# Two attentions with transposed value products, an output product with one sum per attention, and later value transposes in the delta rule

## Chip, cores and metric

The kernel runs on 1 core of one Trainium2 chip. The metric is the device time of one execution in microseconds (us), the median over runs; lower is better. All times are of this one core.

## The reference

Two transformer layers run one after the other on 256 tokens of width 1024, all in float32. What the change touches:

```python
h = rmsnorm(x, g_mix_pre); proj = h @ w_in
y_fox = forgetting_attention(fq, fk, fv, f_logit)            # 8 heads of 64
y_chk = chunked_relpos_attention(cq, ck, cv, rel_bias)       # 8 heads of 64
y = concat([rmsnorm(y_fox.reshape(S, 512), g_fox_out), rmsnorm(y_chk.reshape(S, 512), g_chk_out)])
x = x + rmsnorm(y @ w_out, g_mix_post)
h = rmsnorm(x, g_mem_pre)
x = x + rmsnorm(memory_cross_attention(h, mem_n, ...), g_mem_post)   # 4 heads of 256, ends with @ w_mo
h = rmsnorm(x, g_ff_pre); x = x + rmsnorm(square(relu(h @ w_ff1)) @ w_ff2, g_ff_post)
```

Both attentions of the first line are causal: a softmax over at most 256 keys, then probabilities times values. The second layer has a chunked gated delta rule (8 heads of 128, two chunks of 128 here), an indexer with top-k that masks a second attention (8 heads of 128, named DSA below), gates, an output product and a feed-forward part.

## The kernel before

Every large product is split into three float32r matmuls (`mm3`: high part by high part, high by low, low by high). The stationary and moving operands are tiles with 128 partitions; tokens are handled as two halves of 128 (`A` and `B` in the code, half 0 and half 1). Weights come in units of 512 KB by a DMA from the SP queue into `raw`; ScalarE (ACT) casts `whi`, VectorE (DVE) subtracts to `wlo`. Products with names `gt` give a transposed result (features on partitions, 256 columns), `gn`, `gs` and `mo` a natural one (tokens on partitions, 512 columns), `acc` is the second feed-forward product.

The order of the instructions is made while the program is written out. `Kern` keeps a modelled clock of TensorE and modelled end times of the other engines. Small chains of work (attention heads, norms, evacuations) are generators, called sides. A side yields the tiles it needs, a number of us to wait, a bank of PSUM, or other sides. After each piece of a product `tick` (L261) lets those sides go on whose inputs the model says are ready; `finish` (L272) empties sides at once, whether or not their inputs are near. The result is a fixed order on each engine, which the chip then follows with semaphores. PSUM has 8 banks, and `nb` counts them.

The places that the change and the prediction touch, by the names of the code:

- `attn_pv` (L671): per head three fp32 products with the transposed probabilities `pt` (128x128) stationary and the head's 64 value columns moving, into the natural bank `o`. In the trace each fp32 product has two records.
- `head_pairs` (L862): for two heads at a time scores, softmax, three transposes of `p` (`tb<-ident,p`), a copy `pt` on DVE, then `attn_pv`.
- `out_norm` (L842), once per attention: divides `o` by the softmax sums, squares for the norm, scales by the gain, and four transposes per half (`tb<-ident,y`) through `chain_xt` to the split operand `yt`.
- Output product: `gemm_n_skew(k, yt, 2, ev, ...)` (L990), names `gs`; its post chain `chain_post` (L498) makes the norm, the residual sum `x`, the next norm's `xg` and eight transposes per half (`tb<-ident,xg`) into `xb`. The memory's value product `gemm_n_inter` (`gn`, L991) follows, and then the query product of the memory attention (`gt`).
- Memory attention `mem_head`: scores `ms`, transposes of `mp`, the copy `mpt`, value products `ops`, split `xhi`, `xlo`; then the product with `w_mo` (`mo`, L1043 on).
- Second layer: `chain_v` transposes the values `vc`; `gdn` and `gdn_o` are the delta rule (`wp`, `kp`, `qp`, `op_`), which run among the heads of DSA (`s`, `p`, `pt`, `ao`).

Of the kernel before, what the change touches and what calls it, by code (L numbers as in the profile page):

```python
# [38 lines left out]
def hs(half):  # L39
    return slice(half * P, half * P + P)  # L40
# [454 lines left out]
    yield from chain_xt(k, xt, half, xg, rs)  # L495


def chain_post(k, half, y, gpost, x_old, x_new, gpre, xt):  # L498


    nc = k.nc
    c = lambda t, j: t[:, j * 512:j * 512 + 512]
    yield y
    if gpost is not None:
        ss = mean_sq(k, y, D)
        yg = k.t4([P, D], name="yg")
        for j in range(2):
            nc.vector.tensor_tensor(c(yg, j), y[j], c(gpost, j), op=OP.mult)
        k.put(2)
# [17 lines left out]
    yield rs  # L527
    yield from chain_xt(k, xt, half, [c(xg, 0), c(xg, 1)], rs)


# [178 lines left out]
def block1(k, x, mem, w_in, b_fgt, rel, g_fox_out, g_chk_out, w_out, g_mix_pre, g_mix_post,  # L709
# [123 lines left out]
    gemm_t(k, ht, 512, ev)  # L833


    y = [k.t4([P, D], name="y") for _ in range(2)]
    yt = XS(k)
    gfc = k.t4([P, 2, 512], name="gfc")
# [3 lines left out]
    def out_norm(o, sums, col, g):  # L842

        def half(qt):
            yy = y[qt][:, col:col + 512]
            rs = k.small(8, "rsum")
            nc.vector.reciprocal(rs, sums[:, qt])
            nc.vector.tensor_tensor(yy.rearrange("p (h d) -> p h d", h=8),
                                    o[qt].rearrange("p (h d) -> p h d", h=8), bc(rs, 64), op=OP.mult)
            k.put()  # L850
            ss = mean_sq(k, [yy[:, :256], yy[:, 256:]], 512)
            nc.vector.tensor_tensor(yy, yy, g, op=OP.mult)
            yield ss
            r = rstd_col(k, ss, 512)
            yield r
            yield from chain_xt(k, yt, qt, [yy], r, col // 512)
        yield from join([k.add(half(qt), rank=0) for qt in range(2)])

    def hs64(j):
        return slice(j * 64, j * 64 + 64)  # L860

    def head_pairs(scores, weights, v, o):  # L862
        def rest(h, s):
            p = yield from weights(h, s)
            pt = yield from attn_transpose(k, p, nc.vector.tensor_copy)
            c = slice(h * 64, h * 64 + 64)
            attn_pv(k, pt, v[:, 0, c], v[:, 1, c], o[0][:, c], o[1][:, c])

        def pair(i):
            s = yield from scores(i)  # L870
            yield from join([k.add(rest(2 * i + j, s[j])) for j in range(2)])
        return lanes(k, pair, 4, 3)

    def fox():
        yield from join([s_f])
        o = []
        for _ in range(2):
            o.append((yield from k.get(name="o")))
        sums = k.keep([P, 2, 8], "fsums")

        def scores(i):

            yield fq[:, i], fk[:, i]
            s = []
            for _ in range(2):
                s.append((yield from k.get((P, 4, P), "s")))
            for j in range(2):
                k.mm(flat(s[j])[:, 0:384], sel[:, 2 * i + j], flat(ncum), True, False)
                k.mm(s[j][:, 0], k.identb, k.maskb, False, False)
                k.mm(s[j][:, 2], k.identb, k.maskb, False, False)  # L890
            for j in range(2):
                hp = hs64(j)
                k.mm(s[j][:, 0], fq[hp, i, :P], fk[hp, i, :P], False, False)
            for j in range(2):
                hp = hs64(j)
                k.mm(flat(s[j])[:, P:384], fq[hp, i, P:], fk[hp, i], False, True)
            return s

        def weights(h, s):
            yield s  # L900
            nmx = k.small(2, "nmx")
            nc.vector.tensor_reduce(nmx[:, 0:1], s[:, 0], AX.X, OP.max, negate=True)
            nc.vector.tensor_reduce(nmx[:, 1:2], flat(s)[:, P:384], AX.X, OP.max, negate=True)
            p = k.t2([P, 3, P], name="p")
            softmax_exp(k, p, s, nmx, sums, h)
            k.put()
            return p

        yield from join(head_pairs(scores, weights, fv, o))
        yield o  # L910
        yield from out_norm(o, sums, 0, gfc[:, 0])

    s_fox = k.add(fox())

# [12 lines left out]
    def chk():  # L927
        o = []
        for _ in range(2):
            o.append((yield from k.get(name="o")))  # L930
        sums = k.keep([P, 2, 8], "csums")

        def scores(i):
            yield cq[:, i], ck[:, i]
            s = []
            for _ in range(2):
                s.append((yield from k.get((P, 4, P), "s")))
            for j in range(2):
                hp = hs64(j)
                k.mm(s[j][:, 0], cq[hp, i, :P], ck[hp, i, :P])  # L940
            for j in range(2):
                hp = hs64(j)
                k.mm(flat(s[j])[:, P:384], cq[hp, i, P:], ck[hp, i])
            return s

        def weights(h, s):
            r = rb[h // 4][:, h % 4]
            yield s
            mx = k.small(2, "mx")
            lg = k.t2([P, 3, P], name="lg")  # L950
            nc.vector.tensor_tensor_reduce(lg[:, 0], s[:, 0], r[:, P:], 1.0, 2 * NEG, OP.add, OP.max, mx[:, 0:1])
            nc.vector.tensor_tensor_reduce(flat(lg)[:, P:], flat(s)[:, P:384], r, 1.0, 2 * NEG, OP.add, OP.max,
                                           mx[:, 1:2])
            k.put()
            nmx = k.small(2, "nmx")
            nc.vector.tensor_scalar(nmx, mx, -1.0, None, op0=OP.mult)
            p = k.t2([P, 3, P], name="p")
            softmax_exp(k, p, lg, nmx, sums, h)
            return p

        yield from join(head_pairs(scores, weights, cv, o))
        yield o
        yield from out_norm(o, sums, 512, gfc[:, 1])

    s_chk = k.add(chk())

# [19 lines left out]

    x1 = x0
    ht = XT(k)
    ev, st = post_chain(gpo, x0, x1, gmp, ht)
# [50 lines left out]
    x2 = x1  # L1040
    ht = XT(k)
    ev, st2 = post_chain(gmo, x1, x2, gfp, ht)
    parts = {}  # L1043
    for half in range(2):
        ps = [k.bank(name="mo") for _ in range(2)]
        for js, iis in ((0, (0, 1, 2)), (1, (0, 1, 2)), (0, (3,)), (1, (3,))):
            if iis == (3,):
                k.finish(st[3])
            for i in iis:
                if half == 0:  # L1050
                    while (js, i) not in parts:
                        n = len(parts)
                        parts[n // 4, n % 4] = k.part()
                        k.held += 1
                else:
                    k.drop()
                mm_n(k, ps[js:js + 1], ot, half, parts[js, i], 2 * i)
        ev(half, 0, ps[0:1])
        ev(half, 1, ps[1:2])


    gfo2, gnx = gain(k, g_ff_post), gain(k, next_gain)
# [105 lines left out]
def block2(k, x3, ht, st, out, conv_w, norm_mlp_g):  # L1168
# [735 lines left out]
```

## Time and profile before

| what | value |
|---|---|
| median of 3 runs | 884.3 us (883.33 to 884.74) |
| the profiled execution itself | 884.03 us |
| its span from first to last instruction | 882.1 us |
| mean granted clock of TensorE | 1.000 |
| PE (matmuls) busy | 870.4 us, 99% |
| DVE busy | 603.5 us, 68% |
| ACT busy | 465.3 us, 53% |
| POOL busy | 89.2 us, 10% |

An engine's idle time costs only where TensorE then waits. A matmul's busy time runs past the start of the next one, since matmuls are pipelined; what a matmul costs the program is the distance from its start to the start of the next one, and that is how the rows of a timeline are read here.

### The profile page before, as it was taken

The page shows a single profiled execution, that of the slowest core. Times are in us where ns is not written, and L with a number is a line of the kernel's source. Part 1 is how long each engine was busy: PE and PEld are TensorE (multiplying, and loading weights), DVE is VectorE, ACT ScalarE, POOL GpSimd, SP SyncE. Part 2 cuts the span into 40 slices and gives each one's busy share as a digit, 9 for nine tenths or more (in the row PEclk, how much of TensorE's full clock was granted, in tenths as well). Part 3 has the DMA queues.
Part 4 walks back from the last instruction along what each step waited for, and adds up shares of the span by engine and source line. Part 5 has one row for each costly group of instructions (what it writes and reads, how often), then busy time and mean ns, then how long its engine had stood idle before and what let it go on. Part 6 is the DMA issues. An engine that isn't in the chain of part 4 may idle for free.

```text
span 882.1 us, 13900 instructions
## 1 busy us (share of the span) xinstructions
PE 870.4 (99%) x5320; PEld 754.0 (85%) x5320; DVE 603.5 (68%) x1061; ACT 465.3 (53%) x837; POOL 89.2 (10%) x148
## 2 busy tenths in 40 slices
PE   7999999999999999999999999999999999999998
PEld 6979998799788888888798899988977888888887
DVE  5675664765687667664768999879567786666661
ACT  6574654554476444443648664553765564444440
POOL 3100010200020000000100138600010000000000
PEclk9999999999999999999999999999999999999999
DMA  8982436473387666654553586485235587666521
GB/s 268 294 246 77 144 120 239 119 262 99 94 242 218 207 201 191 191 191 146 172 161 97 143 188 182 97 230 155 71 95 173 165 252 200 191 191 191 192 96 48
DMA packets 162612, 150.82 MB, mean 171 GB/s; under 512 B 20081, under 2 KB 127217, under 8 KB 162546
## 3 DMA queue, kind: packets, MB, share of 16 engines
q1 hardware_dynamic: 161970, 148.88, 56.9%
q10 hardware_dynamic: 576, 1.05, 0.4%
q8 instruction: 42, 0.69, 0.3%
q14 instruction: 24, 0.20, 0.1%
HBM read 148.08 MB, written 1.84 MB: 170 GB/s over the span
## 4 chain that ended last, share of the span: by engine, by line
PE 90%; DVE 4%; ACT 4%; DMA 1%; issue 1%; POOL 0%; ACTq 0%; DVEq 0%; POOLq 0%
PE gt L212 33%; PE acc L212 20%; PE gn L212 12%; PE gs L212 11%; PE tb L225 3%; PE mo L212 3%; DVE wlo L96 2%; PE o L212 1%; ACT whi L96 1%; PE s L212 1%; PE ops L212 1%; PE ms L212 1%; ACT p L96 1%; DMA raw<-in_w_out_dram 1%; PE qp L212 1%
## 5 line engine op out<-in xcount | busy, mean ns | idle before, releaser
L96 DVE TENSOR_TENSOR wlo<-raw,whi 128x1024 fp32r<-128x1024 f32 (+1 forms) x263 | 315.9, 1224 | 107.9 <-ACT whi L96 98.8
L96 ACT CAST whi<-raw 128x1024 fp32r<-128x1024 f32 (+1 forms) x264 | 269.4, 1048 | 61.0 <-DMA raw<-in_w_in_dram 28.8
L212 PE MATMUL gt<-xb,whi 128*128 128x256 f32 (+1 forms) x1152 | 276.1, 322 | 0.0
L212 PE MATMUL gt<-xb,wlo 128*128 128x256 f32 x768 | 215.0, 280 | 0.0
L212 PEld LDWEIGHTS gt<-xb,whi 128*128 128x128 f32 x1152 | 189.9, 188 | 17.2 <-issue 0.3
L212 PEld LDWEIGHTS gt<-xb,wlo 128*128 128x128 f32 x768 | 144.7, 188 | 0.3
L212 PE MATMUL acc<-wlo,uh 128*128 128x512 f32 (+1 forms) x288 | 106.2, 369 | 0.0
L212 PE MATMUL acc<-whi,ul 128*128 128x512 f32 (+1 forms) x288 | 106.2, 369 | 0.0
L212 PE MATMUL acc<-whi,uh 128*128 128x512 f32 (+1 forms) x288 | 106.1, 368 | 0.0
L212 PE MATMUL gn<-whi,xb 128*128 128x512 f32 x256 | 90.2, 408 | 0.0
L212 PE MATMUL gs<-whi,xb 128*128 128x512 f32 (+1 forms) x288 | 86.3, 375 | 0.5 <-ACT xb L96 0.5
L212 PEld LDWEIGHTS acc<-whi,uh 128*128 128x128 f32 x288 | 54.2, 188 | 10.1
L212 PEld LDWEIGHTS acc<-whi,ul 128*128 128x128 f32 x288 | 54.1, 188 | 9.7
L212 PEld LDWEIGHTS acc<-wlo,uh 128*128 128x128 f32 x288 | 54.1, 188 | 9.5
L96 ACT COPY r<-gt 128x256 f32<-128x256 f32 x48 | 17.8, 370 | 84.0 <-PE gt L212 84.0
L212 PEld LDWEIGHTS gs<-whi,xb 128*128 128x128 f32 x288 | 51.9, 188 | 10.8 <-ACT xb L96 1.0
L212 PEld LDWEIGHTS gn<-whi,xb 128*128 128x128 f32 x256 | 48.2, 188 | 10.9 <-issue 1.0
L96 DVE TENSOR_TENSOR r<-gt,r 128x256 f32<-128x256 f32 x48 | 20.3, 423 | 49.7 <-ACT r L96 48.9
L212 PE MATMUL gs<-wlo,xb 128*128 128x512 f32 (+1 forms) x144 | 53.4, 371 | 0.8 <-DVE wlo L96 0.7
L96 POOL TENSOR_SCALAR ms<-ss 128x1 f32<-128x1 f32 x20 | 9.2, 459 | 422.1 <-ACT junk L96 422.0
L212 PE MATMUL gn<-wlo,xb 128*128 128x512 f32 x128 | 50.3, 393 | 0.0
L96 DVE SCALAR_TENSOR_TENSOR cy<-gt,cw,cy 128x255 f32<-128x255 f32 (+2 forms) x72 | 29.1, 474 | 4.7 <-ACT cy L96 4.6
(379 smaller groups left out, 1215.8 us busy)
## 6 DMA issues: line engine op xcount, KB each, us to landing
raw<-in_w_in_dram SPq DMA_DIRECT2D x84, 512.0 KB, 4.7
raw<-in_w_ff_dram SPq DMA_DIRECT2D x64, 512.0 KB, 4.7
raw<-in_w_mlp_up_dram SPq DMA_DIRECT2D x32, 512.0 KB, 5.6
raw<-in_w_mlp_down_dram SPq DMA_DIRECT2D x32, 512.0 KB, 3.4
raw<-in_w_out_dram SPq DMA_DIRECT2D x16, 512.0 KB, 3.8
raw<-in_w_mk_dram SPq DMA_DIRECT2D x8, 512.0 KB, 5.0
raw<-in_w_mv_dram SPq DMA_DIRECT2D x8, 512.0 KB, 4.0
raw<-in_w_mq_dram SPq DMA_DIRECT2D x8, 512.0 KB, 4.9
```

The costliest lines, as they stand in the source:

```text
L96: f(*args, **kw)
L212: self.nc.tensor.matmul(out, lhsT, rhs, start=start, stop=stop)
L225: self.nc.tensor.transpose(out, in_, self.ident[:n, :n])
```

## The change

Four things, with the diff cut to its core:

1. Value products of the first two attentions come out transposed. `p` is divided by its sum before it is transposed, and `attn_pv_t` takes the values (128 keys by 64) as the stationary operand and `pt` as the moving one; the two heads of a pair write rows 0 to 63 and 64 to 127 of the same bank. So `o` has features on partitions and needs no transposes: `out_norm` scales it by the gain (now a column of 8 numbers per partition, loaded by two small DMAs in place of two broadcasts) and splits it into `yt`. The norm's factor per token is made with two products by a column of ones (`ssp`) and kept as `rso`.
2. The output product keeps one bank for each attention (`gs`, four banks per half), and `out_sum` adds the two with their factors `rso`. Its transposes for half 0 are put off by 3 us of the modelled clock.
3. The product with `w_mo` does half 1's first piece before the pieces that need the last memory head.
4. `chain_v` waits 2.5 us of the modelled clock before each group of transposes.

```diff
+def attn_pv_t(k, pts, v, i, o):
+    for b, (q, p0, p1) in enumerate(((slice(0, S), 0, 2), (slice(P, S), 2, 3))):
+        for j in range(2):
+            c = slice((2 * i + j) * 64, (2 * i + j) * 64 + 64)
+            k.mm(o[j * 64:j * 64 + 64, q], v[:, b, c], flat(pts[j][:, p0:p1]), b == 0, b == 1)
...
-    nc.sync.dma_start(gfc[:, 0], bcast_rows(g_fox_out, 512))
-    nc.sync.dma_start(gfc[:, 1], bcast_rows(g_chk_out, 512))
+    for t, g in enumerate((g_fox_out, g_chk_out)):
+        nc.sync.dma_start(gfc[:, 4 * t:4 * t + 4], bass.AP(tensor=g.tensor, offset=g.offset, ap=[[1, P], [P, 4]]))
...
+    def out_norm(o, t):
+        yield o
+        sq = [k.t2([P, 2, S], name="sqo") for _ in range(2)]
+        for b in range(2):
+            nc.scalar.activation(sq[b], o[b], AF.Square, scale=512 ** -0.5)
+            for m in range(2):
+                g, kt = gfc[:, 4 * t + 2 * b + m:4 * t + 2 * b + m + 1], 2 * b + m
+                nc.scalar.activation(yt.hi[t][:, kt], o[b][:, m], AF.Copy, scale=g)
+                nc.vector.scalar_tensor_tensor(yt.lo[t][:, kt], o[b][:, m], g, yt.hi[t][:, kt].bitcast(F32),
+                                               op0=OP.mult, op1=OP.subtract)
+        k.put(2)
+        nc.vector.tensor_tensor(sq[0], sq[0], sq[1], op=OP.add)
+        nc.vector.tensor_tensor(sq[0][:, 0], sq[0][:, 0], sq[0][:, 1], op=OP.add)
+        yield sq[0]
+        yield 3.0
+        sp = yield from k.get(name="ssp")
+        for half in range(2):
+            k.mm(sp[:, half:half + 1], sq[0][:, 0, hs(half)], k.ones[:, 0:1])
...
+        nc.gpsimd.tensor_tensor(rso[:, t], ms, k.mhalf[:, :2], op=OP.pow)
...
-            p = yield from weights(h, s)
-            pt = yield from attn_transpose(k, p, nc.vector.tensor_copy)
-            c = slice(h * 64, h * 64 + 64)
-            attn_pv(k, pt, v[:, 0, c], v[:, 1, c], o[0][:, c], o[1][:, c])
+            p, sums = yield from weights(h, s)
+            yield sums
+            r = k.small(2, "rsum")
+            nc.vector.reciprocal(r, sums)
+            nc.vector.tensor_scalar(p[:, 0], p[:, 0], r[:, 0:1], None, op0=OP.mult)
+            nc.vector.tensor_scalar(p[:, 1:3], p[:, 1:3], r[:, 1:2], None, op0=OP.mult)
+            yield p
+            yield 1.0
+            pts[h % 2] = yield from attn_transpose(k, p, nc.vector.tensor_copy)
...
-    gemm_n_skew(k, yt, 2, ev, before_4=lambda: k.finish(s_chk))
+    def out_sum(half, j, banks, y):
+        yield banks + [rso]
+        yy = y[:, j * 512:j * 512 + 512]
+        nc.scalar.activation(yy, banks[0], AF.Copy, scale=rso[:, 0, half:half + 1])
+        nc.vector.scalar_tensor_tensor(yy, banks[1], rso[:, 1, half:half + 1], yy, op0=OP.mult, op1=OP.add)
+        k.put(2)
...
+    for half in range(2):
+        for j in range(2):
+            for i in range(4):
...
+                for r in range(2):
+                    k.mm3(banks[i // 2], yt.x(2 * i + r, half), p.at(r, 0, 512), i % 2 == 0 and r == 0,
+                          i % 2 == 1 and r == 1)
...
+    seq = [(A,) + x for x in first] + [(B,) + first[0]] + [(A,) + x for x in last]
+    seq += [(B,) + x for x in first[1:] + last]
...
             yield vc[b]
+            yield 2.5
             tp = yield from transposes(k, [vc[b][:, j, hs(half)] for j in range(4)])
```

How the change moves instructions, at three places. The first is TensorE in the first attention, from the transposes of the first heads' probabilities (`tb<-ident,p`) to a value product (`o`); `gt` is the key product of the second attention that fills in between. Before:

```order
L225 MATMUL tb_855<-ident_94,p_824 128x128 x3
L212 MATMUL gt_828<-xb_97,whi_554 128x256 x2
...
L212 MATMUL gt_828<-xb_97,wlo_555 128x256
L212 MATMUL o_740<-fv_203,pt_838 128x64
L212 MATMUL o_741<-fv_203,pt_838 128x64 x2
L212 MATMUL o_740<-fv_203,pt_851 128x64
L212 MATMUL o_741<-fv_203,pt_851 128x64 x2
```

With the change:

```order
L225 MATMUL tb_933<-ident_94,p_829 128x128 x3
L212 MATMUL gt_834<-xb_97,whi_588 128x256 x2
...
L212 MATMUL gt_834<-xb_97,wlo_589 128x256
L212 MATMUL o_739<-pt_892,fv_203 64x256
L212 MATMUL o_739<-pt_894,fv_203 64x256
L212 MATMUL o_739<-pt_892,fv_203 64x128
L212 MATMUL o_739<-pt_894,fv_203 64x128
```

Six products of 64 columns for a pair of heads became four, of 256 and 128 columns, with `fv` stationary and both heads in one bank.

The second is TensorE at the end of the memory's value product (`gn`), where the transposes of half 1's normed input (`tb<-ident,xg`) stand ahead of the memory's query product (`gt`), which reads them as `xb`. Before:

```order
L225 MATMUL tb_2024<-ident_94,xg_1967 128x128 x4
L212 MATMUL gn_1935<-whi_1897,xhi_472 128x512
...
L225 MATMUL tb_2038<-ident_94,xg_1967 128x128 x4
L212 MATMUL gn_1936<-whi_1897,xhi_472 128x512
L212 MATMUL gn_1936<-wlo_1898,xhi_472 128x512
L212 MATMUL gn_1936<-whi_1897,xlo_474 128x512
L212 MATMUL gt_2059<-xb_1760,whi_1937 128x256 x2
```

With the change:

```order
L212 MATMUL gn_1959<-whi_1931,xlo_474 128x512
L225 MATMUL tb_2074<-ident_94,xg_2021 128x128 x4
L225 MATMUL tb_2081<-ident_94,xg_2021 128x128 x4
L212 MATMUL gt_2098<-xb_1779,whi_1960 128x256 x2
L212 MATMUL gt_2098<-xb_1779,wlo_1961 128x256
```

Nothing of the other product stands any more between the transposes and the first reader of what they make.

The third is ScalarE in the second layer, where the squares of the delta rule's second chunk (`junk` with `s4`, of `qs_`) and the exponentials of DSA's second four heads (`p` with `asum`) meet. Before:

```order
L96 ACTIVATE junk_96,s4_6838<-qs__6733 128x128 x4
L96 ACTIVATE p_6869,asum_6870<-lg_6864,nmx_6867,asc_4974 128x128
L96 ACTIVATE p_6869,asum_6870<-lg_6864,nmx_6867,asc_4974 128x256
...
L96 ACTIVATE junk_96,s4_6929<-qs__6764 128x128 x4
```

With the change:

```order
L96 ACTIVATE junk_96,s4_6898<-qs__6817 128x128 x4
L96 ACTIVATE junk_96,s4_6904<-qs__6819 128x128 x4
L96 ACTIVATE p_6916,asum_6917<-lg_6911,nmx_6914,asc_5013 128x128
L96 ACTIVATE p_6916,asum_6917<-lg_6911,nmx_6914,asc_5013 128x256
```

Both groups of squares now stand ahead of the exponentials; one stood behind them.

## Rows read from the trace of the kernel before

**Rows 1.** The page, busy time of each engine.

```profile
PE 870.4 (99%) x5320; PEld 754.0 (85%) x5320; DVE 603.5 (68%) x1061; ACT 465.3 (53%) x837; POOL 89.2 (10%) x148
```

**Rows 2.** Waits of TensorE: who waited for whom, us in total, times, longest.

```profile
PE tb L225 <- DVE xg L96: 1.4, 2, 1.0
...
PE tb L225 <- ACT p L96: 0.7, 3, 0.3
PE mo L212 <- ACT xhi L96: 0.7, 1, 0.7
```

**Rows 3.** Timeline, TensorE, first attention: start us, us, what, count [idle before].

```profile
58.92 0.93 PE L212 MATMUL s<-qk 64*128 64x128 f32 x8
59.77 0.50 PE L212 MATMUL gn<-whi,xb 128*128 128x512 f32 x1
...
81.15 1.45 PE L212 MATMUL o<-fv,pt 128*128 128x64 f32 x12
82.40 0.48 PE L212 MATMUL gt<-xb,whi 128*128 128x256 f32 x2
```

**Rows 4.** The chain that ended last: start us, us that it gave, what, records.

```profile
195.84 1.73 PE ms L212 x8
...
256.42 0.87 PE tb L225 x8
...
541.38 1.68 PE ssp L212 x16
...
545.12 0.89 PE qp L212 x8
...
697.13 11.11 PE gs L212 x48
```

**Rows 5.** Timeline of the softmaxes: a wait of TensorE, DVE before it, a scaling.

```profile
68.40 1.55 PE L212 MATMUL o<-fv,pt 128*128 128x64 f32 x12 [0.49 <-DVE pt L96]
...
66.65 1.23 DVE L96 TENSOR_TENSOR wlo<-raw,whi 128x1024 fp32r<-128x1024 f32 x1 [3.22 <-ACT whi L96]
...
206.40 0.35 DVE L96 TENSOR_SCALAR mp<-mp,mrs 128x256 f32<-128x256 f32 x1
```

**Rows 6.** Timeline, TensorE, transposes inside the output product.

```profile
165.57 0.63 PE L225 MATMUL tb<-ident,xg 128*128 128x128 f32 x4 [0.99 <-DVE xg L96]
```

**Rows 7.** Timeline, TensorE, last memory head and the product with w_mo.

```profile
226.92 1.99 PE L212 MATMUL ops<-mpt,mv 128*128 128x256 f32 x8
229.59 0.50 PE L212 MATMUL mo<-whi,xhi 128*128 128x512 f32 x1 [0.68 <-ACT xhi L96]
...
230.31 0.50 PE L212 MATMUL mo<-whi,xlo 128*128 128x512 f32 x1
```

**Rows 8.** Timeline, TensorE and DVE, eight transposes with their reader right behind.

```profile
425.44 1.04 PE L225 MATMUL tb<-ident,xg 128*128 128x128 f32 x8
426.72 0.50 PE L212 MATMUL gs<-whi,xb 128*128 128x512 f32 x1 [0.24 <-ACT xb L96]
...
427.44 0.73 PE L212 MATMUL gs<-whi,xb 128*128 128x512 f32 x2
...
426.70 1.29 DVE L96 TENSOR_TENSOR xb<-tb,xb 128x512 fp32r<-128x512 f32 x2 [2.87 <-ACT xb L96]
```

**Rows 9.** Timeline, DVE, memory attention, one copy of transposed probabilities.

```profile
204.76 0.42 DVE L96 COPY mpt<-tb 128x256 f32<-128x256 f32 x1
```

**Rows 10.** Timeline, ScalarE and TensorE, delta rule among DSA's heads.

```profile
644.01 0.31 ACT L96 ACTIVATE junk<-qs__6733 128x128 bf16<-128x128 f32 x1 [1.33 <-DVE qs__6733 L96]
...
645.52 0.19 ACT L96 ACTIVATION_READ_ACCUMULATOR junk<-qs__6733 128x1 f32 x1
646.96 0.49 ACT L96 ACTIVATE p<-lg,nmx,asc 128x128 f32<-128x128 f32 x1 [1.25 <-DVE nmx L96]
...
649.38 0.44 PE L225 MATMUL tb<-ident,p 128*128 128x128 f32 x2 [0.26 <-ACT p L96]
```

**Rows 11.** DMA issues by target: count, KB each, median us to landing.

```profile
gfc<-in_g_chk_out_dram SPq DMA_DIRECT2D x1, 256.0 KB, 8.3
```

More of the change, by code (lines that the diff above doesn't have):

```diff
@@ L495, in chain_norm, with chain_post @@
     yield from chain_xt(k, xt, half, xg, rs)
-def chain_post(k, half, y, gpost, x_old, x_new, gpre, xt):
+def chain_post(k, half, y, gpost, x_old, x_new, gpre, xt, nbanks=2, later=0.0):
     nc = k.nc
@@ L527, in chain_post @@
     yield rs
+    if later:
+        yield later
     yield from chain_xt(k, xt, half, [c(xg, 0), c(xg, 1)], rs)
@@ L833, in block1 @@
     gemm_t(k, ht, 512, ev)
-    y = [k.t4([P, D], name="y") for _ in range(2)]
     yt = XS(k)
-    gfc = k.t4([P, 2, 512], name="gfc")
-    nc.sync.dma_start(gfc[:, 0], bcast_rows(g_fox_out, 512))
-    nc.sync.dma_start(gfc[:, 1], bcast_rows(g_chk_out, 512))
[L842 to L857, printed above, removed]
+    gfc = k.keep([P, 8], "gfc")
@@ L877, in fox @@
         for _ in range(2):
-            o.append((yield from k.get(name="o")))
-        sums = k.keep([P, 2, 8], "fsums")
+            o.append((yield from k.get((P, 2, S), name="o")))
         def scores(i):
@@ L929, in chk @@
         for _ in range(2):
-            o.append((yield from k.get(name="o")))
-        sums = k.keep([P, 2, 8], "csums")
+            o.append((yield from k.get((P, 2, S), name="o")))
         def scores(i):
@@ L956, in weights @@
             nc.vector.tensor_scalar(nmx, mx, -1.0, None, op0=OP.mult)
[L957 to L959 removed]
+            p, sums = k.t2([P, 3, P], name="p"), k.small(2, "sums")
+            softmax_exp(k, p, lg, nmx, sums[:, :, None], 0)
+            return p, sums
         yield from join(head_pairs(scores, weights, cv, o))
         yield o
[L963 removed]
+        yield from out_norm(o, 1)
     s_chk = k.add(chk())
@@ L988, in block1, with out_post @@
     ht = XT(k)
-    ev, st = post_chain(gpo, x0, x1, gmp, ht)
-    gemm_n_skew(k, yt, 2, ev, before_4=lambda: k.finish(s_chk))
+    st = {}
+    def out_sum(half, j, banks, y):
[4 more added lines that the diff above has]
+        k.put(2)
+    def out_post(half, sums, y):
+        yield from join(sums)
+        yield from chain_post(k, half, [y[:, :512], y[:, 512:]], gpo, x0[half], x1[half], gmp, ht, nbanks=0,
+                              later=3.0 * (half == A))
+    parts = []
+    for half in range(2):
+        y, sums = k.t4([P, D], name="y"), []
+        for j in range(2):
+            banks = []
+            for i in range(4):
+                if half == 0:
+                    parts.append(k.part())
+                    k.held += 1
+                else:
+                    k.drop()
+                if i % 2 == 0:
+                    banks.append(k.bank(name="gs"))
+                if (half, j, i) == (0, 0, 2):
+                    k.finish(s_chk)
+                p = parts[4 * j + i]
+                for r in range(2):
+                    k.mm3(banks[i // 2], yt.x(2 * i + r, half), p.at(r, 0, 512), i % 2 == 0 and r == 0,
+                          i % 2 == 1 and r == 1)
+                    k.tick()
+            sums.append(k.add(out_sum(half, j, banks, y), rank=-1))
+        st[half] = k.add(out_post(half, sums, y), rank=-1)
+        k.tick()
     gemm_n_inter(k, mt, lambda half, ps: nc.scalar.copy(mv[half][:, 1], ps[0]))
@@ L1042, in block1 @@
     ev, st2 = post_chain(gmo, x1, x2, gfp, ht)
[L1043 to L1059, printed above, removed]
+    parts, mo = {}, {}
+    first = [(js, i) for js in range(2) for i in range(3)]
+    last = [(0, 3), (1, 3)]
+    seq = [(A,) + x for x in first] + [(B,) + first[0]] + [(A,) + x for x in last]
+    seq += [(B,) + x for x in first[1:] + last]
+    for half, js, i in seq:
+        if (half, js, i) == (A, 0, 3):
+            k.finish(st[3])
+        if (half, js) not in mo:
+            mo[half, js] = k.bank(name="mo")
+        if half == A:
+            while (js, i) not in parts:
+                n = len(parts)
+                parts[n // 4, n % 4] = k.part()
+                k.held += 1
+        else:
+            k.drop()
+        mm_n(k, [mo[half, js]], ot, half, parts[js, i], 2 * i)
+        if (js, i) == (1, 3):
+            for j in range(2):
+                ev(half, j, [mo[half, j]])
     gfo2, gnx = gain(k, g_ff_post), gain(k, next_gain)
```

24 lines of the change are left out of this document (17 added, 7 removed).

## The prediction

> **What bounds the kernel now.** I read the page's busy times first, then TensorE's waits, then the chain that ended last, then timelines of the places that the change touches. TensorE is busy for 870.4 of 882.1 us [rows 1], and its listed waits are short: 1.4 us for `xg`, 0.7 each for `p` and `xhi` [rows 2]. So the time is the length of TensorE's list of instructions plus a few waits. DVE and ACT have room as a whole [rows 1] and matter only where TensorE stands and waits for one piece of theirs. Each term below is therefore time on TensorE: records that go or come, and waits that go or come. I count distances from start to start, since the busy times of matmuls overlap.
>
> **Value products.** Before, two heads take 12 records, 81.15 to 82.40, so 1.25 us [rows 3]; eight such pairs make 10.0 us. After, a pair has eight records: four of 256 columns and four of 128. No trace of this kernel has two products side by side with all 128 rows and 64 columns each, so I bound it. One after another they cost what the fp32 products of those lengths cost: 1.73 / 8 = 0.216 us with 256 columns (`ms`) and 0.89 / 8 = 0.111 with 128 (`qp`) [rows 4], 4 x 0.216 + 4 x 0.111 = 1.31 us a pair, 10.5 us in all: a loss of 0.5. Fully side by side it is half, 5.2 us: a gain of 4.8. The nearest row is the scores of a pair: the same eight records of the same lengths, two heads on the two halves of the array's rows. They take 58.92 to 59.77, 0.85 us [rows 3], where one after another would be 1.31, so they overlap, with some 0.2 us of loss on entering or leaving. I take 0.85: 6.8 us, a gain of **3.2**.
>
> The Trainium skill (TensorEngine Tiling (Array Packing), Theoretical Speedup) gives a stationary operand of 64 columns a factor of up to 2, by which this term would be 5.2 us instead of 6.8; no row here has column tiles alone, and the row tiles stay below that factor.
>
> **Transposes of y, and the norm's sums.** Sixteen transposes go: eight cost 0.87 us [rows 4], so 1.75. Four products by a column of ones come, eight records; sixteen cost 1.68 [rows 4], so 0.84. Net gain **0.9**. The second two follow the last value product by 30 products of 512 columns at 11.11 / 48 = 0.231 us [rows 4], so 6.9 us. In it ACT and DVE have about 4 us of squares, splits and sums to do, estimated from 0.35 us for 256 columns [rows 5]: covered, unless more than two weight splits of 1.23 us [rows 5] get in front.
>
> **The wait of the output product's transposes.** It was 0.99 us [rows 6], because the transposes stood 33 products behind their half's last one and DVE's `xg` was late. They now stand 51 products behind it, 4.2 us more at 0.231. Gain **1.0**. The two evacuations that `out_sum` adds per block are on ACT and DVE and lie beside these products; a bank is wanted again only four blocks of 12 products later.
>
> **The product with w_mo.** From the start of `ops`, 226.92, eight records of 0.216 end at 228.65; the third `mo` then could start at 229.11 and starts at 230.31 [rows 7]: 1.2 us lost while ACT and DVE split `ops`. Now one group of three products, 0.7 us, stands in between. Gain **0.7**.
>
> **More work on DVE per head.** Each head gets a reciprocal and two scalings before its transposes; the 256-column one costs 0.35 us [rows 5], so some 0.7 us a head and 11 us in all, with DVE idle 3.2 us at a time in this stretch [rows 5]. DVE's list now puts the third pair's maxima and a weight split behind the scalings of the first pairs, so `pt` of the first pair comes about 0.7 us later, while TensorE has been given 18 products more before it needs it. Walking through the rows I find waits of about 1.0 us where there were 0.5 [rows 5], and the short waits for `p` in the second attention (0.2 of the 0.7 in [rows 2]) go. Loss **0.3**; from a gain of 0.7 (all waits gone) to a loss of 1.5.
>
> **The gains.** Two broadcasts of 256 KB [rows 11] become two DMAs of 2 KB in 4-byte pieces on the same place of the SP queue. Their first reader is the first `out_norm`, behind eight heads that run from 58.92 to 82.40 [rows 3]; the landing took 8.3 us [rows 11]. Nothing.
>
> **Transposes with their reader right behind.** This speaks against the change, at two places. Half 1's eight transposes ahead of the memory's query product had groups of three products between them; now none. Such a block is in the trace: transposes at 425.44, eight of 0.109, so a reader could start at 426.31; it starts at 426.72, and DVE's low part of the first half ends at 426.70 + 0.65 = 427.35 [rows 8]. The query product needs the low part in its second matmul, 0.12 us in: 427.35 - 426.43 = **0.95** lost. At the start of the first feed-forward part the reader needs it in its third matmul, which starts at 427.44 instead of 425.44 + 0.87 + 0.46 = 426.77 [rows 8]: 0.7 lost; half 0's transposes there also come closer to their reader, 0.2 more: **0.9**. Each lies between 0.3, where the tiles are early, and 1.3, where a weight split stands in front.
>
> **Last piece of the memory attention.** `ops` of the third head now follows its transposes directly (there were nine products between); it waits for the copy `mpt`, which takes 0.42 us by itself [rows 9]; with two engines in a row the same pattern loses 0.95, as above. Loss **0.65**, between these ends.
>
> **Delta rule and DSA.** The later value transposes cost nothing by themselves: the order has them inside long products, where nothing waits for them soon. But the order of the rest shifts with them. ACT's two groups of squares now both precede the exponentials of DSA's second four heads. A group takes 644.01 to 645.71, 1.7 us, and TensorE already waits for `p` here [rows 10]. At best the squares are over before the maxima are there, and the waits for `p` go, a gain of 0.5 (twice the row's 0.26). At worst the exponentials come later by a whole group and a weight split in front of it, 1.7 + 1.23 [rows 5], so 2.9 lost. I take a loss of **1.0**, nearer the good end, because TensorE's own delay lets the other engines catch up.
>
> **The sum.** -3.2 - 0.9 - 1.0 - 0.7 + 0.3 + 0.95 + 0.9 + 0.65 + 1.0 = -2.0. The profiled execution took 884.03 us, so 882.0; the median of the runs lies 0.3 above it, so **882.3 us**.
>
> **Rivals.**
>
> *The columns do not overlap, and each change of mode drains.* Place: the eight value products. Price: 1.31 us a pair plus the 0.2 that the scores lose, 8 x 1.51 = 12.1 us instead of 6.8, 5.3 worse: 887.6, slower than before. It decides from 1.10 us a pair on, where the forecast's 2.0 are used up. Against it: the scores overlap in the same form [rows 3]. For it: nothing in the trace shows columns doing so. Chance 0.08. The Trainium skill (TensorEngine Tiling (Array Packing), Key Properties) has the drain: a change of mode, not of the tile, empties TensorE; the scores' 0.2 [rows 3] agree with a short one.
>
> *The delta rule's tail loses all it can*, 2.9 instead of 1.0: 884.2, no change. For it: ACT's list, and the waits already there [rows 10]. Against it: DVE and ACT both have to come late. Chance 0.22.
>
> *The uncertain terms go well*: columns fully side by side (1.6 more) and no loss in the tail (1.0): 879.7. For it: both are ends that the rows allow. Against it: the scores, of the same form, do not reach the full overlap [rows 3]. Chance 0.20.
>
> That the change does not do what it says is no case here: the order shows the transposes gone and the new ones in place.
>
> **How the numbers follow.** The forecast has 0.50, within about 1 us. A measurement of this kernel can tell 0.2%, 1.8 us, from no change, so faster begins at 882.5: all of the third rival and some six tenths of the forecast, 0.51, rounded to 0.52. Slower begins at 886.1: the first rival and a little of the second, 0.09. The rest, 0.39, is no change that can be told. The range reaches from the good case a little below its middle, 879.3, to 885.8 above the tail's worst; the drained columns lie outside. The forecast's own range is 881.0 to 883.4.
>
> **What would show it.** In the profile after: a pair of value products within 0.85 us, records of its two heads starting within some 0.01 us of each other (right), or more than 0.2 apart (first rival). No wait at the output product's `tb<-xg`; a wait of `gt` for `xb` of about 0.9 behind its transposes, of `ops` for `mpt` of some 0.6, of the first feed-forward `gs` for `xb`. Waits of `tb` for `p` in the delta rule's tail: longer than before by about 1 us in all if I am right, by 2.9 for the second rival. The prediction is wrong if TensorE's waits change little in sum but the time falls by over 4 us, or if a wait for `wlo` appears in the first attention, where I let DVE's new work pass for nearly nothing.

## The result and the profile after

The changed kernel takes 889.39 us in the median of 5 runs (888.13 to 889.56), the kernel before 883.96 (5 runs): slower by a ratio of 1.0057, 95% interval [1.0043, 1.0071]. The forecast was 882.3, the range 879.3 to 885.8; slower had a chance of 0.09.

The profiled execution took 889.56 us, its span is 887.8, 5.7 above before. The page's busy times, to be held against [rows 1]:

```profile
PE 871.8 (98%) x5280; PEld 750.2 (84%) x5280; DVE 613.1 (69%) x1107; ACT 466.0 (52%) x833; POOL 79.8 (9%) x142
```

TensorE has 40 records fewer and is busy 1.4 us longer. To see where, I took from its timeline the start of the first record of each stage, in both traces, and compared the lengths of the stages. The last column has the terms of the prediction that fall into each.

| stage (up to the first record of the next) | before, us | after, us | difference | predicted |
|---|---|---|---|---|
| start to the first scores `s<-qk` | 58.92 | 59.13 | +0.21 | 0 |
| both attentions, to the output product's first `gs` | 86.73 | 81.77 | -4.96 | -4.2 |
| output product and second value product, to the memory's first `gt` | 36.25 | 40.05 | +3.80 | +1.0 with the next row |
| memory query product and attention, to the first `mo` | 34.17 | 36.04 | +1.87 | |
| product with w_mo, to the feed-forward part's first `gs` | 28.68 | 27.60 | -1.08 | -0.7 |
| first feed-forward product, to its first `gt` | 24.34 | 27.02 | +2.68 | +0.9 |
| on to the delta rule's first `wp` | 350.05 | 350.67 | +0.62 | +1.0 with the next row |
| delta rule's tail with DSA, to the next `gs` | 40.54 | 43.52 | +2.98 | |
| on to the last matmul | 219.01 | 218.50 | -0.51 | 0 |

The gains came, a little larger than forecast. Three stretches lost far more than forecast. TensorE's waits in the profile after, the answer to [rows 2]:

```profile
PE tb L225 <- DVE xg L96: 3.3, 3, 2.3
PE tb L225 <- ACT p L96: 2.0, 4, 1.3
PE gs L212 <- DVE wlo L96: 1.4, 2, 0.8
...
PE ops L212 <- DVE mpt L96: 0.5, 1, 0.5
PE gt L212 <- DVE xb L96: 0.3, 1, 0.3
```

The wait for `xg` that was to go (0.99 in [rows 6]) is one of 2.3, and that for `p` has grown from 0.7 to 2.0.

**The standstill at 164 us.** DVE's timeline in the stretch ahead of half 0's transposes (start us, us, what, count, idle before):

```profile
160.17 1.29 DVE L96 TENSOR_TENSOR xg<-x,gain 128x512 f32<-128x512 f32 x2
162.12 2.36 DVE L96 TENSOR_TENSOR wlo<-raw,whi 128x1024 fp32r<-128x1024 f32 x2 [0.67 <-ACT whi L96]
164.40 0.74 DVE L96 SCALAR_TENSOR_TENSOR y<-gs,rso,y 128x512 f32<-128x512 f32 x1
165.06 1.22 DVE L96 TENSOR_TENSOR wlo<-raw,whi 128x1024 fp32r<-128x1024 f32 x1
166.19 0.87 DVE L96 TENSOR_SCALAR xg<-xg,rs 128x512 f32<-128x512 f32 x2
```

`rs`, the norm's factor, is there at 162.27 (POOL's power starts at 161.70 and takes 0.57), 1.7 us earlier than before. But the scaling of `xg` by it stands behind three weight splits and a piece of `out_sum`, and starts 3.9 us after `rs`. Before, `rs` was there at 163.93, one split stood in between, and the scaling started 1.0 us after it:

```profile
163.80 1.23 DVE L96 TENSOR_TENSOR wlo<-raw,whi 128x1024 fp32r<-128x1024 f32 x1 [0.68 <-ACT whi L96]
164.95 0.88 DVE L96 TENSOR_SCALAR xg<-xg,rs 128x512 f32<-128x512 f32 x2
```

TensorE's timeline in the profile after, with the products behind the wait:

```profile
166.73 0.66 PE L225 MATMUL tb<-ident,xg 128*128 128x128 f32 x4 [2.34 <-DVE xg L96]
...
167.95 0.63 PE L212 MATMUL gn<-whi,xhi 128*128 128x512 f32 x1
168.38 0.63 PE L212 MATMUL gn<-wlo,xhi 128*128 128x512 f32 x1
...
171.33 0.39 PE L212 MATMUL gn<-whi,xhi 128*128 128x512 f32 x1
171.56 0.40 PE L212 MATMUL gn<-wlo,xhi 128*128 128x512 f32 x1
```

From 167.95 on, products of 512 columns start 0.43 us apart instead of 0.23, until 171.33. The windows of that stretch say why (PEclk is the third column from the right):

```profile
165.00:166.00 1.00, 0.00 (x0) 0.00 (x0) 1.00 (x2) 1.00 (x2) 0.00 (x0) 1.00 1.08 326
...
168.00:169.00 1.00, 1.00 (x4) 0.81 (x3) 1.00 (x3) 0.67 (x4) 0.00 (x0) 0.50 0.93 262
...
171.00:172.00 1.00, 1.00 (x5) 0.83 (x4) 0.75 (x2) 0.85 (x1) 0.47 (x1) 0.86 1.07 285
```

The granted clock is 0.50 there, the lower of its two levels (1.2 of 2.4 GHz), behind a standstill; the trace of before has no such place. A second one follows the waits for `p`, at 656 to 659 us:

```profile
656.00:658.00 2.00, 2.00 (x7) 1.26 (x6) 0.26 (x1) 2.00 (x7) 1.63 (x2) 0.50 0.00 0
```

Of the five runs, one had a mean clock of 1.000 (888.13 us), one 0.998 (888.65) and three 0.996 (889.39 to 889.56).

**The tail.** ScalarE's timeline, the answer to [rows 10]:

```profile
649.52 0.31 ACT L96 ACTIVATE junk<-qs__6817 128x128 bf16<-128x128 f32 x1 [4.53 <-DVE qs__6817 L96]
...
652.56 0.31 ACT L96 ACTIVATE junk<-qs__6819 128x128 bf16<-128x128 f32 x1
...
652.87 0.48 ACT L96 ACTIVATE p<-lg,nmx,asc 128x128 f32<-128x128 f32 x1
```

Eight squares now stand ahead of the first exponential: 649.52 to 652.87, 3.35 us. DVE had the first maxima ready by 650.8:

```profile
650.61 0.16 DVE L96 TENSOR_TENSOR nmx<-mx,nasc 128x2 f32<-128x2 f32 x1
```

**The start of the feed-forward part.** DVE again, half 1's norm:

```profile
248.78 2.35 DVE L96 TENSOR_TENSOR wlo<-raw,whi 128x1024 fp32r<-128x1024 f32 x2
251.04 1.41 DVE L96 SCALAR_TENSOR_TENSOR x<-yg,rs,x 128x512 f32<-128x512 f32 x2
...
254.34 1.23 DVE L96 TENSOR_TENSOR wlo<-raw,whi 128x1024 fp32r<-128x1024 f32 x1 [0.68 <-ACT whi L96]
255.48 0.78 DVE L96 TENSOR_TENSOR r<-r 128x512 f32<-128x512 f32 x1
256.18 1.31 DVE L96 TENSOR_TENSOR wlo<-raw,whi 128x1024 fp32r<-128x1024 f32 x1
257.41 0.90 DVE L96 TENSOR_SCALAR xg<-xg,rs 128x512 f32<-128x512 f32 x2
```

Two splits stand ahead of `x`, and two more, with `r` between them, ahead of the scaling. Before, it was one split ahead of `x`, and two without `r` ahead of the scaling:

```profile
246.76 1.21 DVE L96 TENSOR_TENSOR wlo<-raw,whi 128x1024 fp32r<-128x1024 f32 x1
247.89 1.41 DVE L96 SCALAR_TENSOR_TENSOR x<-yg,rs,x 128x512 f32<-128x512 f32 x2
...
251.18 2.46 DVE L96 TENSOR_TENSOR wlo<-raw,whi 128x1024 fp32r<-128x1024 f32 x2 [0.68 <-ACT whi L96]
253.56 0.94 DVE L96 TENSOR_SCALAR xg<-xg,rs 128x512 f32<-128x512 f32 x2
```

TensorE waits in this stretch for `wlo` (0.8) and for `xg` (0.5); before it waited for neither.

### The profile page after: what moved, and what is told of

Read it like the earlier page. It is cut to its first block, busy times and chain, and to the rows that moved or that the text cites. A ratio compares the mean times of both kernels' runs of the same rounds, so it can differ in the third digit from the quotient of the medians.

```text
span 887.8 us, 13856 instructions
## 1 busy us (share of the span) xinstructions
PE 871.8 (98%) x5280; PEld 750.2 (84%) x5280; DVE 613.1 (69%) x1107; ACT 466.0 (52%) x833; POOL 79.8 (9%) x142
## 4 chain that ended last, share of the span: by engine, by line
PE 90%; DVE 4%; ACT 3%; issue 1%; DMA 0%; POOL 0%; ACTq 0%; DVEq 0%; POOLq 0%
PE gt L212 33%; PE acc L212 20%; PE gn L212 12%; PE gs L212 11%; PE tb L225 3%; PE mo L212 3%; DVE wlo L96 2%; PE s L212 1%; ACT junk L96 1%; ACT whi L96 1%; PE ops L212 1%; PE o L212 1%; PE ms L212 1%; PE ao L212 1%; PE yp L212 0%
## 5 line engine op out<-in xcount | busy, mean ns | idle before, releaser
L96 POOL TENSOR_SCALAR ms<-ss 128x1 f32<-128x1 f32 x16 | 6.9, 432 | 351.4 <-ACT junk L96 351.3
L212 PEld LDWEIGHTS gs<-wlo,xb 128*128 128x128 f32 x144 | 27.2, 189 | 6.7 <-DVE wlo L96 2.5
```

Of the source, the lines that this page charges most:

```text
L96: f(*args, **kw)
L212: self.nc.tensor.matmul(out, lhsT, rhs, start=start, stop=stop)
```

## Experiments

Theory: each loss comes from one edit's place in an in-order list (the `later=3.0` of the output product, the order of the product with w_mo, the 2.5 us of the value transposes), and the standstills make the clock fall as well. The rivals are named in each expectation. Times are medians; the kernel before ran beside them at 883.8 to 883.95.

**e1: the standstill filled, first try.**

```diff
 def transposes(k, srcs, n=P, fill=0):
     ps = yield from k.get((P, 4, P), "tb")
+    for j in range(fill):
+        k.nc.tensor.matmul(ps[:, j % 4], k.ident, k.ident, start=True, stop=True)
```

> The changed kernel with 22 idle fp32 matmuls (128 columns, 0.11 us each, 2.4 us) issued on TensorE into the transposes' own bank, directly ahead of half 0's first four transposes of `xg`, where TensorE stood still for 2.5 us. Nothing of the computation changes. Theory (the standstill itself costs TensorE its clock): the transposes start as late as before the edit, but the granted clock stays at 1.00 behind them; the products of 512 columns there keep 0.23 us instead of 0.43, which gives back about 1.7 us: 887.7 for the median. Rival (the clock falls for another reason, DVE and the DMAs being at their fullest here): clock 0.50 from about 168 to 171 us as in the changed kernel, 889.4 or a little more.

891.06 us, ratio 1.0079 [1.0065, 1.0093]. Inconclusive: each of the 22 is two records, so they took 4.91 us instead of the 2.4 expected and held the transposes up themselves. The clock stayed at 1.00 behind them, but it also did in the profiles of e3 to e6, with the standstill (2.35 us there) left as it was. The fall is a matter of the single execution; only a count over runs can tell (e9).

**e2: half 0's `xg` scaled before the delay**, which is 5.0 instead of 3.0.

```diff
     if later:
-        yield later
+        for j in range(2):
+            nc.vector.tensor_scalar(c(xg, j), c(xg, j), rs, None, op0=OP.mult)
+        rs = None
+        yield later
```

> The changed kernel with half 0's two scalings of `xg` issued as soon as `rs` is there, and only the transposes held back (by 5.0 instead of 3.0). On DVE the scalings then stand behind two weight splits instead of behind three and an `out_sum` piece; the transposes stand one group of three products later than in the changed kernel. Theory (the delay was laid on the scalings too, and the splits that got in front make them late): the wait of the transposes for `xg` falls from 2.5 us to under 0.3, the clock stays at 1.00 there, so 2.5 + 1.7 = 4.2 us come back: 885.2. Rival (DVE and ACT have too much work in this stretch whatever the order): the wait comes back at half 1's transposes or at the memory's query product, and at most 2 us are gained: 887.4 or more.

890.59 us, 1.0073 [1.0061, 1.0086]: no gain. The wait for half 0 is gone, and half 1's transposes, at 179.47, wait instead. TensorE's waits of e2, and the windows around that place:

```profile
PE tb L225 <- DVE xg L96: 5.4, 4, 2.8
```

```profile
176.00:180.00 4.00, 1.21 (x8) 0.74 (x8) 3.16 (x4) 2.54 (x4) 0.71 (x2) 1.00 0.20 59
180.00:184.00 4.00, 3.60 (x18) 3.07 (x17) 3.07 (x4) 3.83 (x5) 0.00 (x0) 0.61 0.98 254
```

The rival holds: what half 0 no longer waits for, half 1 does (2.8 us, behind two splits again), and the clock falls there. That the delay held the scaling back too is not the whole cause. No run took the delay itself away.

**e3: the value transposes without their delay.**

```diff
             yield vc[b]
-            yield 2.5
```

> The changed kernel without the 2.5 us by which the transposes of the delta rule's values are emitted later; nothing else. Theory (this delay alone shifts ACT's list in the delta rule's tail, so that eight squares stand ahead of DSA's exponentials): ACT's list has four squares, three pairs of exponentials and then four squares again, as in the kernel before; the waits for `p` fall from 2.0 us to about 0.7, the clock stays at 1.00 there, and the stretch from the softmax scores to the next projection loses its 3.7 us: 885.7. Rival (the tail is late because all of the program's timing has moved, not because of this delay): the waits for `p` and the fall of the clock stay, 888.5 to 889.5.

886.24 us (10 runs), 1.0023 [1.0014, 1.0032], 3.2 less than the changed kernel. The tail's stage takes 40.51 us (before 40.54, after 43.52). ScalarE's timeline in e3:

```profile
647.00 0.18 ACT L96 ACTIVATION_READ_ACCUMULATOR junk<-qs__6772 128x1 f32 x1
648.43 0.49 ACT L96 ACTIVATE p<-lg,nmx,asc 128x128 f32<-128x128 f32 x1 [1.24 <-DVE nmx L96]
...
654.12 0.31 ACT L96 ACTIVATE junk<-qs__6803 128x128 bf16<-128x128 f32 x1
```

Four squares, the exponentials, then the other four. The theory holds: this one line made the whole loss of the tail.

**e4: the product with w_mo in the old order.**

```diff
-    seq = [(A,) + x for x in first] + [(B,) + first[0]] + [(A,) + x for x in last]
-    seq += [(B,) + x for x in first[1:] + last]
+    seq = [(h,) + x for h in (A, B) for x in first + last]
```

> The changed kernel with the product with w_mo in the order of the kernel before (all of half 0, then half 1). Theory (the new order is what puts two weight splits ahead of half 1's `x` and two more pieces ahead of its `xg` on DVE at the start of the first feed-forward part): the 2.7 us lost between the end of the product with w_mo and the first transposed product of the feed-forward part shrink to under 0.5, the wait behind `ops` returns (about 1.1 us); net 1.0 to 1.5 us less than the changed kernel, 888.1. Rival (DVE is late there because of the earlier stalls, not because of this order): only the wait behind `ops` returns, 890.5.

887.12 us, 1.0036 [1.0023, 1.0048]. The feed-forward part's first product takes 24.41 us (before 24.34, after 27.02), the product with w_mo 28.66 (before 28.68, after 27.60). DVE at the same place as above:

```profile
247.03 1.22 DVE L96 TENSOR_TENSOR wlo<-raw,whi 128x1024 fp32r<-128x1024 f32 x1
248.16 1.41 DVE L96 SCALAR_TENSOR_TENSOR x<-yg,rs,x 128x512 f32<-128x512 f32 x2
...
253.84 0.93 DVE L96 TENSOR_SCALAR xg<-xg,rs 128x512 f32<-128x512 f32 x2
254.70 0.68 DVE L96 TENSOR_TENSOR r<-r 128x512 f32<-128x512 f32 x1
```

One split stands ahead of `x` again, and `r` behind the scaling. The theory holds: the new order gained 1.1 us and lost 2.6 behind it. The rest of e4's gain in its profile is the clock, which did not fall at 168 us: that stage, with the same standstill, took 38.87 us there (38.86 in e3), 1.2 less than in the changed kernel. So 1.2 us is the price of this fall.

**e5: another order of the value products.** Both blocks of one head, then both of the other.

```diff
-    for b, (q, p0, p1) in enumerate(...):
-        for j in range(2):
+    for j in range(2):
+        for b, (q, p0, p1) in enumerate(...):
```

> The changed kernel with the eight records of a pair of value products in another order: both blocks of the one head, then both of the other, instead of the two heads in turn. All other engines keep their lists, and the result is the same. Theory (a pair takes 0.80 us instead of 1.31 because neighbouring records lie on different columns of the array and overlap): only the middle two records still overlap, a pair takes 1.1 to 1.3 us, and the eight pairs lose 2.4 to 4 us: 891.8 to 893.4. Rival (the rate comes from elsewhere, as from the fp32 products' short stationary operand, and the order does not matter): 0.80 us a pair, 889.4.

888.23 us, 1.0052 [1.004, 1.0065]. The theory about neighbours falls, and the rival's 0.80 comes true. TensorE's timeline, one pair in the changed kernel and the same pair in e5:

```profile
82.73 0.87 PE L212 MATMUL o<-pt,fv 128*64 128x256 f32 x8
83.53 0.55 PE L225 MATMUL tb<-ident,p 128*128 128x128 f32 x3
```

```profile
82.59 0.88 PE L212 MATMUL o<-pt,fv 128*64 128x256 f32 x8
83.40 0.55 PE L225 MATMUL tb<-ident,p 128*128 128x128 f32 x3
```

0.80 us from start to start, and 0.81. In both traces the eight records start in twos, 0.006 us apart in the changed kernel and 0.013 in e5, the four of 256 columns first. So the two heads' products run beside each other in e5 too, and the rival's other source of the rate is not needed. What falls is that they must alternate in the kernel's order. The Trainium skill (TensorEngine Tiling (Array Packing), Key Properties) says that tiles run independently of each other; e5 agrees with it.

**e6: e3 and e4 together.**

> The changed kernel without the delay of the delta rule's values and with the w_mo product in the order of the kernel before, so the two edits that each gained alone, together. Theory (the three losses lie in three separate stretches and add): 889.4 - 3.2 - 2.3 = 883.9, within 0.2% of the kernel before; the stretch of the output product alone still loses 2.6 us. Rival (each of the two gains holds the same fall of the clock, or the planner's order shifts again): 885.5 or more.

884.48 us (11 runs), 1.0007 [0.9998, 1.0016]: the losses add, and nothing is left that can be told from the kernel before. The theory holds, 0.6 us off; 7 of the 11 runs had a mean clock of 0.998, and 4, the profiled one among them, of 1.000. The stage of the output product still takes 38.86 us.

**e7 and e8: the weight splits held back.**

```diff
-            if self.n_split - self.n_used >= 4 and any(s.rank < 0 for s in self.sides):
+            if self.n_split - self.n_used >= self.lim and any(s.rank < 0 for s in self.sides):
```

with `lim` 2 (e7) or 1 (e8) from the output product to the end of its norms, on top of e2's edit and e6. `lim` is how many split parts of weights may stand ready ahead of TensorE while a norm's chain is open.

> As e6, and in the stretch of the output product half 0's `xg` is scaled as soon as `rs` is there, its transposes are held back by 5.0, and the weight splits stop two parts ahead of TensorE instead of four while a norm's chain is open. Theory (it is the splits standing ahead of `xg` and `x` on DVE that make the transposes late, in both halves): no wait over 0.5 us for `xg` in either half, 2 to 2.6 us less than e6: 881.5 to 882. Rival (DVE has too much work there in any order): the time comes back as waits for `wlo` in the second value product or the memory's query product, and e7 is within 0.8 us of e6.

> As e7, with the splits stopped one part ahead. Theory: as e7 for `xg`, half 1's transposes with products between them, 881 to 882. Rival (with one part ahead the splits come too late for TensorE): waits for `whi` or `wlo` of 0.5 to 2 us in the second value product, 883 or more.

e7: 883.70 us, 1.0002 [0.9993, 1.0011]. The output product's stage falls from 38.86 to 36.00 us, as the theory has it, but the next one, memory query and attention, takes 39.57 instead of 36.03. e2 had the early scaling alone and kept a wait of 2.8 us, so it is the held splits that take it away. The rival holds in the sum (0.8 below e6), not in the place it named. TensorE's waits in e7 (that for `xg` lies in the first 30 us, not here):

```profile
PE tb L226 <- DVE mp L96: 2.1, 3, 1.2
PE ms L213 <- ACT mq L96: 1.5, 1, 1.5
...
PE tb L226 <- DVE xg L96: 0.4, 1, 0.4
```

e8: 885.64 us, 1.0024 [1.0015, 1.0032]. With one part the splits come too late: waits of `gn` for `whi` (0.9) and `wlo` (0.8), as its rival said.

**e9: the standstill filled with 11 products, on e6.**

> As e6, with 11 idle fp32 matmuls (two records of 0.11 us each, 2.45 us in all, as measured in e1) on TensorE directly ahead of half 0's transposes of `xg`, where it stood still for 2.5 us. In e6, 7 of 11 runs had a mean clock of 0.998 and took 885.1 us in the middle, the 4 with 1.000 took 883.7. Theory (the standstill makes the clock fall behind it, in some executions and not in others): the transposes start no later than in e6, the mean clock is 1.000 in all or nearly all runs, and the median is 883.7. Rival (the falls have nothing to do with the standstill): about as many runs at 0.998 as in e6, median 884.5.

883.92 us, 1.0004 [0.9995, 1.0013]. TensorE's timeline:

```profile
164.12 2.62 PE L462 MATMUL tb<-ident 128*128 128x128 f32 x22
166.63 0.66 PE L225 MATMUL tb<-ident,xg 128*128 128x128 f32 x4
```

The mean clock was 1.000 in 10 of 11 runs and 0.999 in one, against 0.998 in 7 of 11 in e6. The one at 0.999 is the profiled one, and its clock falls at 881 us, behind the last matmul. So the standstill is what makes the clock fall in e6. The Trainium skill (TensorE: Matmul & The Clock Gate, Why this matters for your kernels) advises against idle gaps of TensorE between bursts of matmuls, since the half clock can come back behind them. e9 agrees in kind; the gap that it fills is shorter than those the page names. The two were run on different chips; on e9's chip e10 and e11 had 0.998 or less in 4 and 6 of 11 runs, so it is not the chip, and falls come without this standstill too. Where in a run they lie is shown for the profiled ones alone. The medians differ by 0.56 us, less than the two intervals can tell apart.

**e10 and e11: fewer splits in a row behind it.** In the memory's query product `k.ls = 4` instead of 6 (the split parts kept ready when no norm's chain is open), with `lim` 3 (e10) or 2 (e11).

> As e7, with the splits held three parts ahead of TensorE in the output product's stretch, and in the memory's query product four parts ahead instead of six, so that DVE's list has four splits in a row ahead of the first `nmx` instead of nine. Theory (what e7 gave back, it gave back because nine splits in a row stood ahead of the memory attention's maxima): the 2.9 us that e7 gained ahead of the query product stay, the stretch from there to the w_mo product takes 35 to 36 us instead of 39.6, and the whole 880.5 to 881.5. Rival (ACT and DVE have too much work from the output product to the w_mo product in any order): the waits move once more, 883 or more.

> As e10 with the splits held two parts ahead in the output product's stretch, so five in a row ahead of the first `nmx` and two more behind it, as in the changed kernel. Theory: as e10, 880.5 to 881.8. Rival: as e10, 883 or more.

e10: 885.83 us, 1.0024 [1.0016, 1.0033], with waits for `xg` (1.5) and `mp` (2.4); e11: 883.53, 1.0003 [0.9994, 1.0012]. In e11 the stages of the output product and the memory attention take 36.00 and 36.44 us, 72.44 together against 74.89 in e6: there the theory is right. But the product with w_mo then takes 30.54 instead of 28.68, with a wait of its last memory head for `mp`. The rival's number stands; the waits move on.

**e12: e11 with the new w_mo order and `lim` 1 to the end of the first feed-forward product.**

> As e11, with the w_mo product in the changed kernel's order again, and the splits held one part ahead of TensorE from there to the end of the first transposed product of the feed-forward part. On DVE the scaling of half 1's `xg` then stands ahead of `r` and of the split that stood ahead of it in the changed kernel. Theory (the new order is worth its 1.1 us as soon as the splits do not stand in front of half 1's chain): no wait over 0.4 us at the start of the feed-forward part, 1 us less than e11, 882.5. Rival (DVE and ACT have no room there either, and held splits come late): waits for `wlo` or `xb` of 1 to 2.5 us in the feed-forward part's first product, 884 to 886.

886.72 us (8 runs), 1.0031 [1.0019, 1.0043]. The first feed-forward product takes 30.41 us; its windows and waits:

```profile
244.00:250.00 6.00, 4.08 (x15) 2.30 (x13) 5.33 (x8) 3.86 (x7) 2.26 (x5) 0.94 0.58 178
250.00:256.00 6.00, 5.53 (x15) 4.36 (x16) 5.56 (x7) 2.59 (x4) 4.22 (x8) 0.50 0.68 200
```

```profile
PE gs L213 <- ACT whi L96: 1.7, 1, 1.7
```

The rival holds in its reason, that held splits come late, but not in the place: the longest wait is for ScalarE's `whi` (1.7), that for `wlo` is 0.5, and the time is 0.7 above its range. The clock falls once more behind these waits. DVE is busy 10.9 of these 12 us.

No version beat the kernel before beyond the measurement. Four cannot be told apart from it, with the transposed value products in: e6, e7, e9 and e11.

## Why the prediction was wrong, point by point

- **What bounds the kernel** was read rightly: the time is TensorE's list plus its waits. But "DVE and ACT have room as a whole" hid that DVE has next to none beside the norms, where it also makes the weights' splits: it was busy 10.89 of the 12 us from 158 to 170 before, and 7.22 of the 7.50 from 163.50 to 171.00 after. Room there is, but earlier. From the output product to the memory's first `gt` DVE was busy 22.84 of 36.25 us before and 25.09 of 40.10 after, and ahead of the norms ScalarE, whose casts DVE's splits need, stood idle for 7.5 us:

```profile
153.80 1.05 ACT L96 CAST whi<-raw 128x1024 fp32r<-128x1024 f32 x1 [7.51 <-PE gs L212]
```

- **Value products**, forecast 0.85 us a pair: 0.80. Right, and so is the sign of the records starting together (0.006 us apart). The drained columns, the rival with the right sign, did not happen.
- **Transposes of y, the norm's sums, DVE's work per head**: the attentions' stage gained 4.96 us, forecast 4.2. Right; the short waits went, as the good end of that term had it.
- **The gains**, nothing: the two small DMAs are issued at 49.4 and 50.2 us and land 5.2 us later at most; their first reader starts at 85.7. Right.
- **The wait of the output product's transposes**: this step failed first. "They now stand 51 products behind it ... Gain 1.0" counted products on TensorE and held `xg` where it was. On DVE's list the scaling stands behind three splits and `out_sum`; the step did not follow that list. With the splits held back (e7) the wait goes, and the stage takes 36.00 us. Of the 5.67 us of the two stages, against 1.0 forecast, the wait accounts for 1.35 more (2.50 from start to start, 1.15 before) instead of 1.0 less, and the clock for 1.2.
- **The product with w_mo**, gain 0.7: 1.08. Right, but
- **the start of the feed-forward part**, loss 0.9: 2.68. This step was mis-sized, with the wrong cause. I priced eight transposes with their reader right behind, as in [rows 8]; the trace has one split more ahead of half 1's `x` and `r` ahead of its scaling. Both come from the w_mo order: with the old one the stage takes 24.41 (e4).
- **Transposes ahead of the memory's query product, and the last piece of the memory attention**: `ops` at 0.65 and `gt` at 0.95 were right in kind (by its own rows the second is 427.35 - 426.43 = 0.92, which changes nothing). The stage from the first `gt` on lost 1.87, of which a wait of `gt` of some 0.5 us and waits for `mp` and `mpt` of 0.8; the rest, some 0.6, is not explained.
- **Delta rule and DSA**: this step failed last. The mechanism is the second rival's, eight squares ahead of the exponentials, but I took a loss of 1.0 "because TensorE's own delay lets the other engines catch up"; nothing of the kind happened. The tail lost 2.98 us, and e2's execution, where the clock did not fall in the tail, has 42.35 us for it, 1.8 above before. So 1.8 is the list's loss and 1.2 the clock's; that the sum is the rival's 2.9, which had no clock in it, is luck.
- **The clock** was in no term. In the profiled execution it fell twice, 1.2 us each, 2.4 of the 5.6. Over the runs it counts for less: the one with a mean clock of 1.000 is 1.3 us below the three with 0.996, and at 888.13 it is 4.2 above the kernel before, outside the range without any fall.

The answer to the forecast's test is plain: "No wait at the output product's `tb<-xg`" is wrong by 2.3 us. Its other signs came: `gt` waits for `xb` (0.6), `ops` for `mpt` (0.5). The waits of `tb` for `p` are 1.3 longer in sum, near my own number though the stage lost 2.98: the listed waits alone would have hidden the rest.

What stays open: whether taking work off DVE in the stretch from the output product on (the second half of `out_sum`, say, on another engine) would keep the attentions' 5 us. The experiments only moved its work in order; none took any away, and none made splits earlier, in the 7.5 us in which ScalarE stood idle ahead of the norms. Nor did any run undo the delay of 3.0 us or `out_sum` by itself, so which of the two puts the splits ahead of `xg` is open.

## What to carry to other kernels

When an edit delays a step, find every instruction that goes with it on the other engines' in-order lists, and see what now stands ahead of it there; its distance on the bounding engine says little. Look for the stretches in which the helping engines are full, not for their share of the whole: a gain of 5 us on TensorE was spent in three such places, and of the orders tried here none kept it. And give a standstill of TensorE (2.3 us here) a second price: the products behind it may run at half the clock.

## What was not expected of the hardware

- Behind a wait of 2.3 us TensorE's granted clock fell to 0.50 in the changed kernel's profile and not in those of e3 to e6, which have the same wait; 7 of e6's 11 runs had a mean clock of 0.998, and none with the wait filled (e9). The fall that was measured by itself cost 1.2 us.
- Value products on two halves of the columns overlap in both orders tried: 0.80 and 0.81 us a pair.
- A matmul of two fp32 operands of 128 columns is two records of 0.11 us, so that 22 of them took 4.91 us.
